# One trunk layer on one Trainium2 core: weights times values of both attentions in two matmuls instead of three, halves added by an accumulating DMA

## The chip, the cores and the metric

The kernel runs on one core of a Trainium2 chip. The metric is the device time of one execution in microseconds (us), the median of three runs. The profile is taken from one further execution by the hardware profiler; its times count from the start of its own span. The engines are PE (TensorE; PEld is its weight load), DVE (VectorE), ACT (ScalarE), POOL (GpSimd) and SP (SyncE, which here only issues DMAs).

## The reference, cut to what matters

One decoder layer over 1024 positions: an input projection, four mixers side by side (a state space model, "fox" attention with forgetting, RWKV-7, "sb" stick-breaking attention), a gated merge of the four, an output projection, an MLP. The two attentions are:

```python
# both: 4 heads of 64, S = 1024, query blocks of 128
def _forgetting_attention(q, k, v, f_logit):           # "fox"
    logits = einsum('bqhd,bkhd->bhqk', qb, kf) * scale
    logits = logits + c[query] - c[key]                # c: running sum of log-sigmoid(f_logit)
    probs = softmax(where(kpos <= qpos, logits, -inf))
    return einsum('bhqk,bkhd->bqhd', probs, vf)

def _stick_breaking_attention(q, k, v):                # "sb"
    z = einsum('bqhd,bkhd->bhqk', qb, kf) * scale
    log_rest = where(kpos < qpos, log_sigmoid(-z), 0)
    between = cumsum(log_rest, reverse) - log_rest
    weights = where(kpos < qpos, exp(log_sigmoid(z) + between), 0)
    return einsum('bhqk,bkhd->bqhd', weights, vf)
```

The change is in the last line of each: weights times values.

## The kernel before

Everything is float32 accurate to more bits than one fp32r matmul gives, so each operand is split in two fp32r tiles, a high half (a rounded copy, by ACT) and a low half (the rest, by DVE: `split`), and a product is three matmuls: high by high, low by high, high by low.

The program is one sequence for the PE that a planner in the file (`Driver`) sets: generators emit work, the planner keeps a modelled clock with costs of its own for each engine, and emits what is ready. The PE's order is the order of emission. On DVE and ACT the order is pinned to the planner's modelled start times. SP and POOL, which issue the DMAs and a few memsets, are ordered by the framework. Every engine works its own queue strictly in order. The attentions run in two stages, fox (430 to 591 us of the span) and sb (756 to 939), each with three `worker` generators over 32 items, 4 heads by 8 query blocks (`qb` 7 down to 0). Beside them the PE fills with gate projections and branch merges (`merges`, matmuls named `mm<-t,wh`, `mm<-y,wh` and the like), whose weights ACT and DVE split as they arrive.

One item: scores by PE into PSUM tiles `x` (QS by KH and KL); weights W by DVE and ACT (fox: `ACTIVATE W` is the exponential; sb: ACT writes the sigmoids R and W, DVE scans R); PE transposes W (`x<-cst,W`); ACT writes the high half `PTh`, DVE the low half `WR`; then, for each of the `qb + 1` key blocks, three matmuls into `y[0:64]`, 64 array columns wide with 128 columns streamed: Vh by PTh, Vl by PTh, Vh by WR. ACT copies the sum to `yst` (a pool of two buffers), and SP stores it to `SCR["Y"]` (`scr_Y`) in DRAM, which the merges read back as `wr<-scr_Y`. In sb, POOL writes a single 1 behind each R row (`MEMSET R`).

In the planner's model a DMA reads nothing that is held: `issue("d", ..., outs, [], ...)` has an empty list of inputs, so it takes a `yst` buffer to be free when ACT has written it. On the chip the copy two later waits until the DMA that reads the buffer has landed. A store costs the planner's model `outs[0].nbytes() / 3.6e5 * (1 + more)` on its one DMA resource, with `more` set for an accumulating DMA.

Of the kernel before, what the change touches and what calls it, by code (L numbers as in the profile page):

```python
# [9 lines left out]
F32 = mybir.dt.float32  # L10
F32R = mybir.dt.float32r
BF16 = mybir.dt.bfloat16
AF = mybir.ActivationFunctionType
ALU = mybir.AluOpType
AX = mybir.AxisListType

P = 128
# [299 lines left out]
def body(ctx, tc, I, O, dbg=None):  # L317
    nc = tc.nc
    drv = Driver()
    V, A, G, SY = (Timed(e, drv, k, tc) for e, k in ((nc.vector, "v"), (nc.scalar, "a"), (nc.gpsimd, "g"), (nc.sync, "s")))  # L320
# [22 lines left out]
    def nm(s):  # L343
        uid[0] += 1
        return f"{s}_{uid[0]}"
# [15 lines left out]
    def px():  # L361
        return ps.tile([P, 512], F32, tag="x", name=nm("x"), bufs=5)
# [21 lines left out]
    def split(dst_h, dst_l, src):  # L384
        A.copy(dst_h, src)
        V.tensor_tensor(out=dst_l, in0=src, in1=dst_h.bitcast(F32), op=ALU.subtract)
# [186 lines left out]
    SCR = {}  # L573
# [424 lines left out]
    def attn(pool, which):  # L998
        fox = which == 0
        ops, left = {}, [8] * 4  # L1000
# [6 lines left out]
        made, count = {}, [0] * 4  # L1007

        def operands(tag):
            def stage():  # L1010
                return wpool.tile([P, 512], F32, tag=tag, name=nm("st"), bufs=NRAW if tag == "wr" else 1)
            while jobs and (tag or jobs[0][0] == 0):
                hd, k = jobs.pop(0)
                while hd >= 2 and left[hd - 2]:
                    yield None
                if hd not in made:
                    made[hd] = [pool.tile([P, S], F32R, tag=t, name=nm(t), bufs=2) for t in ("QS", "KH", "KL")]
                    made[hd] += [pool.tile([P, 8, 64], F32R, tag=t, name=nm(t), bufs=2) for t in ("Vh", "Vl")] + [None]
                    if fox:
                        made[hd][5] = pool.tile([P, S], F32, tag="cb", name=nm("cb"), bufs=2)  # L1020
                        G.dma_start(out=made[hd][5], in_=SCR["c"][hd].partition_broadcast(P))
                QS, KH, KL, Vh, Vl, cb = made[hd]
                ct, o64 = hd // 2, (hd % 2) * 64
                if k < 4:
                    h = (0, 1, 1, 0)[k]
                    hs = slice(h * 512, (h + 1) * 512)
                    src = SCR["qk"][which * 4 + ct + 2 * (k % 2 == 0)]
                    t = pool.tile([P, 512], F32, tag="PTh", name=nm("raw"), bufs=4) if hd == 0 else stage()
                    for half in (0, 64):
                        SY.dma_start(out=t[half:half + 64], in_=src[o64:o64 + 64, hs])  # L1030
                    yield 0.1
                    if k % 2 == 0:
                        split(KH[:, hs], KL[:, hs], t)
                    else:
                        A.activation(out=QS[:, hs], in_=t, func=AF.Copy, scale=0.125)
                        V.scalar_tensor_tensor(out=QS[64:128, hs], in0=t[64:128], scalar=0.125, in1=QS[64:128, hs].bitcast(F32),
                                               op0=ALU.mult, op1=ALU.subtract)
                elif fox:
                    t = stage().rearrange("p (a d) -> p a d", d=64)
                    SY.dma_start(out=t, in_=SCR["v"].rearrange("(a p) d -> p a d", p=P)[:, :, hd * 64:hd * 64 + 64])  # L1040
                    yield 0.1
                    split(Vh, Vl, t)
                else:
                    h = k - 4
                    t = stage()[0:64]
                    SY.dma_start(out=t, in_=SCR["qk"][8 + ct, o64:o64 + 64, h * 512:(h + 1) * 512])
                    yield 0.1
                    o = px()
                    for tb in range(4):
                        T.transpose(o[:, tb * 64:(tb + 1) * 64], t[:, tb * P:(tb + 1) * P], ident[0:64, 0:64])  # L1050
                    hv = slice(h * 4, h * 4 + 4)
                    split(Vh[:, hv].rearrange("p a d -> p (a d)"), Vl[:, hv].rearrange("p a d -> p (a d)"), o[:, 0:256])
                count[hd] += 1
                yield 0.1
                if count[hd] == (5 if fox else 6):
                    ops[hd] = made[hd]
            if not jobs:
                ws.cap = NRAW

        def worker():  # L1060
            for n, hd, qb in items:
                while hd not in ops or turn[0] < n:
                    yield None
                QS, KH, KL, Vh, Vl, cb = ops[hd]
                ct, o64 = hd // 2, (hd % 2) * 64
                L = (qb + 1) * P
                qsl = slice(qb * P, (qb + 1) * P)
# [12 lines left out]
                for n0 in range(0, L, 512):  # L1080
                    n1 = min(L, n0 + 512)
                    o = px()
# [27 lines left out]
                for g0 in range(0, qb + 1, 4):  # L1110
                    o = px()
# [3 lines left out]
                WR = pool.tile([P, S if L > 512 else 512], F32R, tag="W" + sz, name=nm("WR"), bufs=2)  # L1115
# [6 lines left out]
                y = px()  # L1122
                for kb in range(qb + 1):
                    ph = pth[kb // 4][:, kb % 4 * P:kb % 4 * P + P]
                    T.matmul(y[0:64, 0:P], lhsT=Vh[:, kb, :], rhs=ph, start=kb == 0, stop=False)
                    T.matmul(y[0:64, 0:P], lhsT=Vl[:, kb, :], rhs=ph, start=False, stop=False)
                    T.matmul(y[0:64, 0:P], lhsT=Vh[:, kb, :], rhs=WR[:, kb * P:(kb + 1) * P], start=False, stop=kb == qb)
                free["W" + sz] += 1
                free["P"] += (L + 511) // 512
                yst = pool.tile([64, P], F32, tag="yst", name=nm("yst"), bufs=2)  # L1130
                A.copy(yst, y[0:64, 0:P])
                SY.dma_start(out=SCR["Y"][1 if fox else 3, ct, o64:o64 + 64, qsl], in_=yst)
                left[hd] -= 1
                if not any(left):
                    finished["fox" if fox else "sb"] = True
# [2 lines left out]
        for tag in ("st", "wr", None, None, None):  # L1138
            drv.add(operands(tag), 1)
        for _ in range(3):  # L1140
            drv.add(worker(), 0)
# [1099 lines left out]
```

## Time and profile before

| | us |
|---|---|
| median of 3 runs (lowest, highest) | 1870.84 (1868.87, 1873.22) |
| the profiled execution: its own time | 1872.88 |
| the profiled execution: its span | 1871.1 |
| PE busy in the span | 1815.3 (97%) |
| fox stage, first 130 us (430 to 560): PE busy | 126.61 |
| sb stage (756 to 945, 189 us): PE busy, DVE busy | 181.20, 154.79 |

The profiled execution's own time is 1.8 us above its span and 2.0 above the median. Busy time of a PE matmul counts from its start to a modelled end, so neighbouring matmuls overlap: the distance between two starts is what one costs in a dense run. "Idle before" in square brackets at a row's end is the engine's wait and what ended it.

### The profile page before, as it was taken

The page shows a single profiled execution, that of the slowest core. Times are in us where ns is not written, and L with a number is a line of the kernel's source. Part 1 is how long each engine was busy: PE and PEld are TensorE (multiplying, and loading weights), DVE is VectorE, ACT ScalarE, POOL GpSimd, SP SyncE. Part 2 cuts the span into 40 slices and gives each one's busy share as a digit, 9 for nine tenths or more (in the row PEclk, how much of TensorE's full clock was granted, in tenths as well). Part 3 has the DMA queues.
Part 4 walks back from the last instruction along what each step waited for, and adds up shares of the span by engine and source line. Part 5 has one row for each costly group of instructions (what it writes and reads, how often), then busy time and mean ns, then how long its engine had stood idle before and what let it go on. Part 6 is the DMA issues. An engine that isn't in the chain of part 4 may idle for free.

```text
span 1871.1 us, 27581 instructions
## 1 busy us (share of the span) xinstructions
PE 1815.3 (97%) x9651; PEld 1479.0 (79%) x9651; DVE 1239.0 (66%) x2596; ACT 717.0 (38%) x1412; POOL 208.5 (11%) x279
## 2 busy tenths in 40 slices
PE   8999999998999999999999998999999999999998
PEld 7877777777888877787877876788888887888876
DVE  8775865616876764688867666766656565866574
ACT  5443343225454212655544125343333343443230
POOL 0331111100000000000000001111111211121000
PEclk9999999999999988999999998999999999999999
DMA  7343223124422412412154128888889898988441
GB/s 254 114 127 102 82 75 95 66 67 143 146 87 81 101 40 59 129 54 70 39 207 150 51 81 226 239 249 231 245 238 251 209 273 258 284 219 220 129 148 46
DMA packets 177948, 275.27 MB, mean 147 GB/s; under 512 B 37760, under 2 KB 59552, under 8 KB 177680
## 3 DMA queue, kind: packets, MB, share of 16 engines
q1 hardware_dynamic: 155488, 226.31, 37.2%
q0 software_dynamic: 22320, 47.18, 12.9%
q8 instruction: 76, 1.25, 0.3%
q14 instruction: 64, 0.52, 0.1%
HBM read 199.76 MB, written 56.89 MB: 137 GB/s over the span
## 4 chain that ended last, share of the span: by engine, by line
PE 58%; DVE 7%; DMA 5%; ACT 2%; issue 1%; SPq 0%; DVEq 0%; ACTq 0%; POOL 0%; POOLq 0%
PE mm L327 28%; PE x L327 28%; DVE R L280 2%; PE x L332 2%; DMA wr<-in_mlp_w2t_dram 1%; DVE sn L280 1%; DVE W L280 1%; DVE tq L280 1%; DMA scr_g<-gs 1%; DVE t L280 1%; DMA wr<-wl 0%; DMA wl<-in_mlp_w_dram 0%; DMA sn<-scr_H 0%; DMA raw<-scr_qk 0%; DVE Z L280 0%
## 5 line engine op out<-in xcount | busy, mean ns | idle before, releaser
L327 PE MATMUL mm<-t,wh 128*128 128x512 f32 x1600 | 512.6, 402 | 3.5 <-ACT th L280 2.2
L327 PEld LDWEIGHTS mm<-t,wh 128*128 128x128 f32 x1600 | 292.7, 190 | 65.6 <-ACT th L280 2.6
L327 PE MATMUL mm<-t,wl 128*128 128x512 f32 x800 | 314.0, 392 | 0.0
L327 PE MATMUL x<-t,wp 128*128 128x512 f32 x1152 | 270.2, 394 | 8.5 <-ACT wp L280 5.0
L327 PEld LDWEIGHTS x<-t,wp 128*128 128x128 f32 x1152 | 218.4, 190 | 57.5 <-ACT wp L280 5.8
L327 PE MATMUL x<-sx,wp 128*128 128x512 f32 x768 | 179.9, 389 | 1.7 <-ACT sx L280 1.5
L327 PEld LDWEIGHTS mm<-t,wl 128*128 128x128 f32 x800 | 151.3, 189 | 33.2
L327 PEld LDWEIGHTS x<-sx,wp 128*128 128x128 f32 x768 | 144.1, 188 | 32.3 <-ACT sx L280 1.9
L280 ACT CAST wh<-wr 128x512 fp32r<-128x512 f32 (+1 forms) x125 | 74.6, 597 | 122.9 <-PE mm L327 93.7
L280 ACT CAST wp<-wr 128x512 fp32r<-128x512 f32 x96 | 59.2, 621 | 139.4 <-DMA wr<-wl 60.5
L280 DVE TENSOR_TENSOR wp<-wr,wp 128x512 fp32r<-128x512 f32 x96 | 65.8, 688 | 69.7 <-ACT wp L280 68.8
L280 POOL TENSOR_TENSOR wl<-wr,wh 128x512 fp32r<-128x512 f32 x50 | 68.9, 1378 | 278.3 <-ACT wh L280 278.1
L327 PE MATMUL mm<-t,wp 128*128 128x512 f32 x384 | 90.1, 390 | 0.0
L327 PE MATMUL mm<-sx,wp 128*128 128x512 f32 x384 | 89.6, 389 | 0.0
L327 PE MATMUL mm<-wo,t 128*128 128x512 f32 x384 | 89.1, 391 | 0.0
L327 PEld LDWEIGHTS mm<-t,wp 128*128 128x128 f32 x384 | 72.5, 189 | 15.3
L327 PEld LDWEIGHTS mm<-sx,wp 128*128 128x128 f32 x384 | 72.1, 188 | 15.0
L327 PEld LDWEIGHTS mm<-wo,t 128*128 128x128 f32 x384 | 71.6, 188 | 14.5
L280 DVE TENSOR_TENSOR wl<-wr,wh 128x512 fp32r<-128x512 f32 (+1 forms) x75 | 47.4, 634 | 36.6 <-ACT wh L280 35.8
L280 DVE TENSOR_TENSOR wp<-wl,wp 128x512 fp32r<-128x512 f32 x64 | 43.8, 688 | 39.6 <-ACT wp L280 39.5
L280 DVE TENSOR_TENSOR wp<-wh,wp 128x512 fp32r<-128x512 f32 x64 | 43.9, 690 | 32.5 <-ACT wp L280 32.5
L280 ACT CAST wp<-wl 128x512 fp32r<-128x512 f32 x64 | 39.5, 620 | 53.5 <-PE x L327 23.9
(380 smaller groups left out, 3207.9 us busy)
## 6 DMA issues: line engine op xcount, KB each, us to landing
wr<-in_w_in_dram SPq DMA_DIRECT2D x110, 256.0 KB
scr_H<-sn SPq DMA_DIRECT2D x100, 256.0 KB
wr<-in_mlp_w_dram SPq DMA_DIRECT2D x84, 256.0 KB
sn<-scr_H SPq DMA_DIRECT2D x84, 256.0 KB
wh<-in_mlp_w_dram SPq DMA_DIRECT2D x56, 256.0 KB
wl<-in_mlp_w_dram SPq DMA_DIRECT2D x56, 256.0 KB
wr<-wl POOLq DMA_DIRECT2D x32, 256.0 KB, 6.2
wl<-wr POOLq DMA_DIRECT2D x32, 256.0 KB, 4.3
```

The source lines that it names most:

```text
L280: r = f(*a, **kw)
L327: return nc.tensor.matmul(out, lhsT=lhsT, rhs=rhs, **kw)
L332: return nc.tensor.transpose(out, in_, idn)
```

## The change

The two value tiles Vh and Vl (64 columns each) become one tile VV of 128 columns, high values left, low values right. PTh is then streamed once against all 128 columns, into all 128 PSUM partitions (0 to 63: Vh by PTh, 64 to 127: Vl by PTh), and WR against the left 64 columns as before. ACT copies 128 partitions instead of 64. SP stores partitions 0 to 63, and a second DMA, issued by POOL with `accum_op=ALU.add`, adds partitions 64 to 127 to the same DRAM rows once the first has landed.

```diff
@@ operands
-                    made[hd] += [pool.tile([P, 8, 64], F32R, tag=t, name=nm(t), bufs=2) for t in ("Vh", "Vl")] + [None]
+                    vv = pool.tile([P, 8, 128], F32R, tag="VV", name=nm("VV"), bufs=2)
+                    made[hd] += [vv[:, :, 0:64], vv[:, :, 64:128], None, vv]
...
-                    split(Vh[:, hv].rearrange("p a d -> p (a d)"), Vl[:, hv].rearrange("p a d -> p (a d)"), o[:, 0:256])
+                    split(Vh[:, hv], Vl[:, hv], o[:, 0:256].rearrange("p (a d) -> p a d", d=64))
@@ worker
                     ph = pth[kb // 4][:, kb % 4 * P:kb % 4 * P + P]
-                    T.matmul(y[0:64, 0:P], lhsT=Vh[:, kb, :], rhs=ph, start=kb == 0, stop=False)
-                    T.matmul(y[0:64, 0:P], lhsT=Vl[:, kb, :], rhs=ph, start=False, stop=False)
-                    T.matmul(y[0:64, 0:P], lhsT=Vh[:, kb, :], rhs=WR[:, kb * P:(kb + 1) * P], start=False, stop=kb == qb)
+                    T.matmul(y[:, 0:P], lhsT=VV[:, kb, :], rhs=ph, start=kb == 0, stop=kb == qb)
+                    T.matmul(y[0:64, 0:P], lhsT=Vh[:, kb, :], rhs=WR[:, kb * P:(kb + 1) * P], start=False, stop=kb == qb,
+                             skip_group_check=True)
                 free["W" + sz] += 1
                 free["P"] += (L + 511) // 512
-                yst = pool.tile([64, P], F32, tag="yst", name=nm("yst"), bufs=2)
-                A.copy(yst, y[0:64, 0:P])
-                SY.dma_start(out=SCR["Y"][1 if fox else 3, ct, o64:o64 + 64, qsl], in_=yst)
+                yst = pool.tile([P, P], F32, tag="yst", name=nm("yst"), bufs=2)
+                A.copy(yst, y[:, 0:P])
+                dst = SCR["Y"][1 if fox else 3, ct, o64:o64 + 64, qsl]
+                SY.dma_start(out=dst, in_=yst[0:64])
+                G.dma_start(out=dst, in_=yst[64:128], accum_op=ALU.add)
```

On POOL the new DMAs stand in the one queue with the memsets of R. This is a stretch of POOL's program early in the sb stage, after the change (before it, the same stretch holds the memsets alone; a number behind a name tells buffers apart):

```order
L280 MEMSET R_8109 128x1
L280 DMA scr_Y<-yst_8103 64x128
L280 MEMSET R_8189 128x1
L280 DMA scr_Y<-yst_8143 64x128
L280 MEMSET R_8219 128x1
L280 DMA scr_Y<-yst_8183 64x128
L280 MEMSET R_8504 128x1
L280 DMA scr_Y<-yst_8213 64x128
L280 MEMSET R_8430 128x1
```

Each accumulating DMA waits there for the store of the same rows, and a memset behind it waits with it.

On ACT the place of the copies among the rest stays as it was for the first head of fox. This is the stretch with its short last blocks, after the change:

```order
L280 COPY yst_4858<-x_4847 128x128
L280 CAST PTh_4868<-x_4862 128x512
L280 CAST wh_4877<-wr_4739 128x256
L280 CAST PTh_4888<-x_4883 128x384
L280 COPY yst_4903<-x_4894 128x128
L280 COPY yst_4925<-x_4918 128x128
L280 ACTIVATE W_4907,sm_4908<-W_4907,sm_4908 128x256
L280 ACTIVATE W_4929,sm_4930<-W_4929,sm_4930 128x128
```

Copies 4903 and 4925 each need a buffer whose last readers are the two DMAs of an item two earlier; the exponentials stand behind them.

From the second head of fox on, the planner's order moves by a few rows on PE, DVE and ACT (sb keeps its order almost wholly). On DVE, where the second head's middle blocks are made ready, it stood like this before (mg is the running merge, WR the low half of the transposed weights):

```order
L280 TENSOR_TENSOR KL_5060<-st_5065,KH_5059 128x512
L280 RECIPROCAL sm_5222<-sm_5222 128x1
L280 TENSOR_SCALAR W_5221<-W_5221,sm_5222 128x512
L280 SCALAR_TENSOR_TENSOR QS_5058<-st_5068,QS_5058 64x512
L280 TENSOR_TENSOR wl_5237<-wr_4905,wh_5236 128x256
L280 SCALAR_TENSOR_TENSOR mg_4372<-th_5105,mm_5115 128x512
L280 SCALAR_TENSOR_TENSOR mg_4373<-th_5243,mm_5247 128x512
L280 TENSOR_TENSOR WR_5267<-x_5259,PTh_5268 128x512
```

And after the change:

```order
L280 TENSOR_TENSOR wl_5193<-wr_4881,wh_5192 128x256
L280 RECIPROCAL sm_5178<-sm_5178 128x1
L280 TENSOR_SCALAR W_5177<-W_5177,sm_5178 128x512
L280 TENSOR_TENSOR KL_5030<-st_5034,KH_5029 128x512
L280 SCALAR_TENSOR_TENSOR QS_5028<-st_5037,QS_5028 64x512
L280 SCALAR_TENSOR_TENSOR mg_4372<-th_5074,mm_5084 128x512
L280 TENSOR_TENSOR WR_5218<-x_5210,PTh_5219 128x512
L280 TENSOR_TENSOR WR_5218<-x_5215,PTh_5222 128x256
```

The split wl moved ahead of W and KL behind it, and the second merge step moved behind the two WR.

## Rows read from the trace of the kernel before

**Rows 1.** From the profile's page: busy time of each engine, and the shares of the chain of work that ended last.

```profile
PE 1815.3 (97%) x9651; PEld 1479.0 (79%) x9651; DVE 1239.0 (66%) x2596; ACT 717.0 (38%) x1412; POOL 208.5 (11%) x279
PE 58%; DVE 7%; DMA 5%; ACT 2%; issue 1%; SPq 0%; DVEq 0%; ACTq 0%; POOL 0%; POOLq 0%
```

**Rows 2.** Busy time by stretch, the fox stage's first 130 us and the sb stage. Columns: the stretch, its length, busy us (instructions) of PE, PEld, DVE, ACT, POOL, the granted PE clock as a share of 2.4 GHz, the DMA share, GB/s.

```profile
430.00:560.00 130.00, 126.61 (x840) 107.62 (x839) 97.11 (x268) 68.34 (x161) 2.17 (x4) 0.97 0.43 129
756.00:945.00 189.00, 181.20 (x1196) 149.28 (x1196) 154.79 (x265) 102.31 (x246) 6.01 (x35) 1.00 0.24 71
```

**Rows 3.** The matmuls of weights times values, by operands. Columns: count, then ns of one (lowest, median, highest), first and last start, and in front of the shape of the streamed operand rows by columns of the array.

```profile
L327 PE MATMUL x<-PTh,Vh x288: 218/222/308, 455.5 to 938.2; 128*64 128x128 f32 x144
L327 PE MATMUL x<-WR,Vh x288: 220/222/308, 455.6 to 938.3; 128*64 128x128 f32 x144
...
L327 PE MATMUL x<-PTh,Vl x288: 220/222/308, 455.5 to 938.3; 128*64 128x128 f32 x144
```

**Rows 4.** PE in order of time: the ends of one run of 24 such matmuls with what stands before and behind it, and the end of another with a pair 128 columns wide behind it. Columns: start, us from start to end, then as above.

```profile
455.24 0.39 PE L327 MATMUL mm<-t,wl 128*128 128x512 f32 x1
455.46 0.22 PE L327 MATMUL x<-PTh,Vh 128*64 128x128 f32 x1
...
456.84 0.22 PE L327 MATMUL x<-WR,Vh 128*64 128x128 f32 x1
456.90 0.45 PE L327 MATMUL x<-KH,QS 128*128 128x512 f32 x1
457.19 0.40 PE L327 MATMUL x<-KL,QS 128*128 128x512 f32 x1
457.42 0.28 PE L327 MATMUL x<-KH,QS 128*128 128x256 f32 x1
...
552.19 0.22 PE L327 MATMUL x<-WR,Vh 128*64 128x128 f32 x1
552.25 0.28 PE L327 MATMUL x<-KH,QS 128*128 128x128 f32 x1
552.36 0.28 PE L327 MATMUL x<-KL,QS 128*128 128x128 f32 x1
552.47 0.69 PE L327 MATMUL mm<-t,wh 128*128 128x512 f32 x2
```

**Rows 5.** DMAs issued by POOL: count, KB of each, median us from issue to landing.

```profile
y<-in_x_dram POOLq DMA_DIRECT2D x8, 512.0 KB, 3.8
scr_v<-vs POOLq DMA_DIRECT2D x8, 128.0 KB, 2.0
cst<-in_consts_dram POOLq DMA_DIRECT2D x1, 144.0 KB, 6.3
```

**Rows 6.** SP's queue at the end of the sb stage: the last two stores of yst, and the first reads of the same rows, which wait for them.

```profile
938.72 1.08 SPq L280 DMA_DIRECT2D scr_Y<-yst  x2
941.24 0.82 SPq L280 DMA_DIRECT2D wr<-scr_Y  x2
```

**Rows 7.** The first head's short blocks in fox, in order of time on SP, ACT and PE: the stores of two items (two issues in one row), the copies two items later, the exponential behind them, and the transposes that need it.

```profile
471.79 1.62 SPq L280 DMA_DIRECT2D scr_Y<-yst  x2
...
475.80 0.26 ACT L280 COPY yst<-x 64x128 f32<-64x128 f32 x1 [0.93 <-PE x L327]
476.62 0.26 ACT L280 COPY yst<-x 64x128 f32<-64x128 f32 x1 [0.56 <-PE x L327]
476.78 0.51 ACT L280 ACTIVATE W<-W,sm 128x256 f32<-128x256 f32 x1
...
478.26 0.38 PE L332 MATMUL x<-cst,W 128*128 128x128 f32 x2
```

**Rows 8.** The same at short blocks of the third head in sb: two stores, the copies two items later, the sigmoid between them, and the transposes.

```profile
886.56 1.23 SPq L280 DMA_DIRECT2D scr_Y<-yst  x2
...
890.12 0.26 ACT L280 COPY yst<-x 64x128 f32<-64x128 f32 x1 [0.29 <-PE x L327]
890.41 0.38 ACT L280 ACTIVATE R<-x 128x256 f32<-128x256 f32 x1
891.64 0.26 ACT L280 COPY yst<-x 64x128 f32<-64x128 f32 x1 [0.57 <-ACT W L280]
...
892.68 0.41 PE L332 MATMUL x<-cst,W 128*128 128x128 f32 x2 [0.26 <-DVE W L280]
```

**Rows 9.** Two of POOL's memsets of R in the same place, with POOL's wait before each.

```profile
888.60 0.10 POOL L280 MEMSET R<- 128x1 f32 x1 [7.68 <-DVE W L280]
892.65 0.10 POOL L280 MEMSET R<- 128x1 f32 x1 [3.95 <-DVE W L280]
```

**Rows 10.** After the sb stage: the split of the branch weights, the matmuls that use them with the sb values read back, and the PE's next wait.

```profile
951.04 0.41 ACT L280 CAST wh<-wr 128x256 fp32r<-128x256 f32 x1 [2.40 <-DMA wr<-in_w_branch_dram]
...
952.77 0.62 PE L327 MATMUL mm<-y,wh 128*128 128x512 f32 x2
...
965.33 0.70 PE L327 MATMUL mm<-y,wh 128*128 128x512 f32 x2 [2.42 <-DVE th L280]
```

**Rows 11.** The PE's longest wait in the fox stage, and the two stretches behind it (columns as in rows 2).

```profile
500.44 1.22 PE L327 MATMUL mm<-y,wh 128*128 128x512 f32 x2 [3.12 <-DVE mg L280]
...
500.00:505.00 5.00, 4.56 (x15) 3.58 (x16) 4.46 (x10) 0.00 (x0) 0.00 (x0) 0.50 0.72 223
505.00:510.00 5.00, 5.00 (x44) 4.66 (x43) 2.35 (x8) 2.40 (x7) 0.00 (x0) 0.83 0.54 151
```

More of the change, by code (lines that the diff above doesn't have):

```diff
@@ L1021, in operands @@
                         G.dma_start(out=made[hd][5], in_=SCR["c"][hd].partition_broadcast(P))
-                QS, KH, KL, Vh, Vl, cb = made[hd]
+                QS, KH, KL, Vh, Vl, cb, _ = made[hd]
                 ct, o64 = hd // 2, (hd % 2) * 64
@@ L1063, in worker @@
                     yield None
-                QS, KH, KL, Vh, Vl, cb = ops[hd]
+                QS, KH, KL, Vh, Vl, cb, VV = ops[hd]
                 ct, o64 = hd // 2, (hd % 2) * 64
```

## The prediction

> **What bounds the kernel now.** I read the page first. PE is busy for 97% of the span and carries 58% of the chain that ended last, more than all other engines together [rows 1]. So a microsecond counts when it is a microsecond of PE: matmuls that take less, or a PE that waits. Then the two stages that the change touches [rows 2]: in the fox stretch PE idles 130 - 126.61 = 3.4 us, in sb 189 - 181.20 = 7.8 us, with DVE at 82%. There is almost no idle time to win back, and what ACT or DVE are late by soon shows on PE, whose order is fixed.
>
> **The matmuls.** The three groups have 288 each, 64 columns wide, 128 streamed [rows 3]. Their 222 ns is a latency. What one costs is the distance of two starts: 24 run from 455.46 to 456.90 [rows 4], 0.060 us each. A key block is 3 x 0.060 = 0.180, all 288 blocks 51.8 us.
>
> After, a block is one matmul 128 columns wide and one 64 wide, both with 128 streamed. The nearest row for the wide one is the score pair KH, KL at 128 streamed: 552.25, 552.36, 552.47 [rows 4], 0.11 each, nearly twice the 64-wide one though it streams as much. So width sets the price here, not the stream. Block: 0.111 + 0.060 = 0.171, saving 0.009 x 288 = **2.6 us**. The ends: if the wide one cost 0.060 as well, 17.3 us saved. If each step from narrow to wide cost extra as it does before a long matmul (456.90 to 457.19 is 0.29, the next 0.23 [rows 4]), 0.06 more a block, 288 x (0.06 - 0.009) = 14.7 us lost. I take 0.171: the short pair behind a narrow run shows 0.06 and 0.11, without an extra.
>
> The Trainium skill speaks against the change twice. "TensorE: Matmul & The Clock Gate", section "LDWEIGHTS (loading the stationary operand)", gives the load as columns over 1.2 ns; as an estimate 53 and 107 ns, so 160 for a block either way, nothing saved. Rows 4 show a little more per matmul than that, 0.060 and 0.11; with nothing saved the sum below is +5.2 instead of +2.6. And "TensorEngine Tiling (Array Packing)", section "Key Properties", says that changing the tiling mode, not just the tile, drains the engine, and the new pair changes width at each matmul. The trace does not show a drain where widths change: 455.24 to 455.46 is 0.22 behind a long matmul, 552.19 to 552.25 is 0.06 [rows 4]. If it drained, 576 changes would each cost the rest of the latency, 0.222 - 0.060, together 93 us.
>
> **ACT's copy and the splits** keep their free size (128 and 512 columns), only partitions and strides change: nothing, and ACT is 38% busy [rows 1] if a few ns were added.
>
> **The accumulating DMA and the two yst buffers.** This is where it can lose. A buffer is free for the copy two later when its last DMA has landed. A store takes about 1.95 us: the second issue of the last pair starts at about 939.3, the read of the same rows goes out at 941.24 [rows 6]. Now the add follows: it waits for that landing, is issued by POOL, and lands. No accumulating DMA is in this trace. Bounds: 2.0 us, a store four times as large from POOL, and 6.3, a load at the kernel's start [rows 5]. An add must read DRAM before it writes, so it lies above the plain store; the read of 512 KB takes 3.8 with its larger transfer. I take 3.0, between those two. So a buffer is held 4.95 us from the store's issue.
>
> Where does that meet a copy? In fox's first head the stores go out at 471.79 and 472.95, so the buffers come free at 476.74 and 477.90; the copies two later ran at 475.80 and 476.62 [rows 7], so they are held by 0.9 and 1.3. In sb's third head a store at 886.56 frees its buffer at 891.51, and the copy at 890.12 [rows 8] is held 1.4. Counted in this way over all 64 copies, seven places are held, by 0.4 to 1.4 us; these two are the first and the last. Together **5.8 us**. At 2.0 two places are left, 0.7 us. At 6.3 each gets 3.3 more and some six others join with about 2: 5.8 + 23 + 12 = 41.
>
> Behind the held copy on ACT wait the exponential (476.78) or the sigmoids (890.41), behind those DVE's work on W, behind that PE's transposes. At 892.68 PE already waits 0.26 us for DVE [rows 8], so a hold there is passed on in full; at 478.26 PE does not wait [rows 7], so some of it is cover. I take four fifths: 4.6 us (ends 0.6 and 33).
>
> **POOL.** Its queue is in order, so memsets of R stand behind adds that wait for their stores. A memset now follows at once on the release of R after waits of 4 to 8 us [rows 9]; the adds ahead of it are due before that release (at 889 the one ahead of 892.65). Nothing; with that cover gone, up to about 2.5 us at each head's end in sb. In fox the loads of cb stand between adds too; each waits for DVE to leave the buffer of two heads earlier, which comes after the adds ahead of it.
>
> **The end of sb.** The read of the finished rows (941.24) waits for the last add, 3 us later, and SP's queue behind it holds the branch weights. Their high half is done at 951.45 and the matmul takes it at 952.77 [rows 10], so 1.3 us are to spare and 1.7 would show. But PE's next wait, 2.42 us at 965.33, is for the gate values th, which do not come from the attention, and takes up most of what PE lost before it. I count a third, **0.6 us** (ends 0 and 3.0). At fox's end the merges that read its rows come much later: nothing.
>
> **The planner.** The matmul terms of its model do not change, but its DMA resource is booked more, and from fox's second head on some rows change places. The longest PE wait of the stage lies there: 3.12 us on a merge step of DVE at 500.44, followed by a granted clock of 0.50 for 5 us and 0.83 for the next [rows 11]. That costs 3.1 + 2.5 + 0.85 = 6.5 us. The new order does the same DVE work ahead of the first merge step, so I count 0, with 6.5 either way.
>
> **Sum:** -2.6 + 4.6 + 0.6 = +2.6 us. On the profiled execution, whose own time is 1872.88, that is 1875.5; it lies 2.0 above the median of the runs, so I forecast **1873.4**, a gain on PE given back by held copies. A difference under 0.2% (3.7 us) can hardly be told from none here.
>
> **The rivals.**
> - *Late add (slower).* The add lands after 4.5 us: seven holds grow by 1.5, some others join with 3 together, 19 us, four fifths of it 15; -2.6 + 15 + 0.6 = +13, 1884. For it: loads from POOL of 3.8 and 6.3 us. Against: the POOL store of 2.0 us, and the add is small. It decides from an add of 3.2 us on, where the net passes 3.7.
> - *No gain on PE.* The block costs what it did: +5.2, 1876.0. Rows 4 leave 9 ns a block, which is little to rely on.
> - *The stall goes.* The new order takes away the wait at 500.44 and the low clock behind it: 1873.4 - 6.5 = 1866.9, with an add of 2.0 us 1862.3. For it: the changed rows are just there. Against: DVE was busy 4.46 of 5 us behind the wait [rows 11], and its work is the same.
> - *A third less.* The wide matmul costs what a narrow one does: -17.3 + 5.2, 1858.7. For it: the same columns are streamed. Against: the pair at 552.25.
> - *A drain at each change of width:* 1873.4 + 93 + 2.6, 1969. Against: the changes in rows 4.
>
> **How the numbers follow.** Forecast 0.42 (1868.8 to 1874.6, nearly all within 0.2%), late add 0.27, no gain 0.05, the stall goes 0.16 (two thirds of it faster by more than 0.2%), a third less 0.07, drain 0.03. Faster: 0.07 + 0.11 = 0.18. Slower: 0.27 + 0.05 + 0.03 and 0.02 from the forecast's upper end, 0.37. Same: 0.45. The range, 1864 to 1887, leaves out the drain, a third less, the lowest of the stall that goes (0.03) and the upper part of the late add (0.07), 0.2 in all.
>
> **What would show it.** Starts of the wide and narrow matmuls 0.17 us apart per block. ACT's copies waiting for DMA scr_Y in some seven places, 0.4 to 1.4 us each, about 5 us after the store of two items before. PE waits for DVE W in sb up from before, by 3 to 4 us. The read of the sb rows 3 us behind its store's landing. POOL's adds landing after about 3 us. I would be wrong if the adds land after more than 4 us, if the distance of starts is not 0.17, or if the wait and the low clock at 500 are gone or have a twin elsewhere.

## The result, and the profile after

The changed kernel takes 1881.61 us (median; 1871.57 to 1891.0), the kernel before, beside it on the same chip, 1872.17 (1857.4 to 1880.94). The ratio is 1.0052, with a 95% interval from 1.0037 to 1.0067: about 9 us slower, inside the range forecast and beyond the 1873.4 that was forecast as likeliest. The profiled execution's own time is 1885.72, its span 1883.9.

The two stages of the change, as in [rows 2], of after:

```profile
430.00:560.00 130.00, 120.29 (x696) 101.07 (x696) 92.95 (x249) 63.43 (x147) 18.77 (x24) 0.97 0.49 133
756.00:945.00 189.00, 175.77 (x1016) 143.87 (x1015) 149.57 (x250) 101.26 (x239) 25.39 (x59) 0.99 0.30 76
```

PE, the first busy column, now idles 9.7 us in the fox stretch and 13.2 in sb, where it idled 3.4 and 7.8. The granted clock, the third column from the right, is what it was to 0.01. So PE isn't slower at its work: it waits more.

One run of weights times values in order of time on PE, of after, which answers to [rows 4] (start, us, then operands, rows by columns of the array, streamed shape):

```profile
459.63 0.39 PE L327 MATMUL mm<-t,wl 128*128 128x512 f32 x1
459.87 0.22 PE L327 MATMUL x<-PTh,VV 128*128 128x128 f32 x1
459.92 0.22 PE L327 MATMUL x<-WR,VV 128*64 128x128 f32 x1
459.98 0.28 PE L327 MATMUL x<-PTh,VV 128*128 128x128 f32 x1
460.09 0.22 PE L327 MATMUL x<-WR,VV 128*64 128x128 f32 x1
...
461.02 0.27 PE L327 MATMUL x<-PTh,VV 128*128 128x128 f32 x1
461.13 0.22 PE L327 MATMUL x<-WR,VV 128*64 128x128 f32 x1
461.19 0.45 PE L327 MATMUL x<-KH,QS 128*128 128x512 f32 x1
```

From 459.98 to 461.19 lie seven blocks, 0.173 us each: 0.11 for the wide matmul, 0.06 for the narrow one. The first wide one of this run costs only 0.05 (459.87 to 459.92); its load had started at 459.64, while the matmul ahead still ran. Over all runs the first wide one costs 0.06 in the median, the others 0.11. Summed, from the first start of each run to the next other matmul, the 288 blocks take 49.5 us; before they took 54.1.

Now ACT's waits over both attentions, of after (us in total, times, longest):

```profile
ACT yst L280 <- DMA scr_Y<-yst: 31.2, 15, 5.7
ACT yst L280 <- PE x L327: 24.4, 21, 2.5
```

The first line did not exist before: in that trace no wait of a yst copy is put down to a DMA. And PE's waits for W in sb (756 to 960), of before and then of after:

```profile
PE x L332 <- DVE W L280: 4.8, 10, 1.0
```

```profile
PE x L332 <- DVE W L280: 9.8, 14, 1.7
```

One hold followed from engine to engine, in sb of after (SP, POOL, ACT, DVE, PE; in brackets the idle time before the row and what ended it):

```profile
896.29 1.23 SPq L280 DMA_DIRECT2D scr_Y<-yst  x2
899.14 0.82 POOL L280 DMA_DIRECT2D scr_Y<-yst  x1 [8.49 <-DVE WR L280]
902.54 0.27 ACT L280 COPY yst<-x 128x128 f32<-128x128 f32 x1 [3.16 <-DMA scr_Y<-yst]
902.70 0.39 ACT L280 ACTIVATE R<-x 128x256 f32<-128x256 f32 x1
903.13 0.29 DVE L280 TENSOR_TENSOR R<-R,cst 128x128 f32<-128x128 f32 x1 [3.16 <-ACT R L280]
904.97 0.41 PE L332 MATMUL x<-cst,W 128*128 128x128 f32 x2 [1.65 <-DVE W L280]
```

The store is issued at 896.29, its add 2.85 us later, and the copy that needs the buffer starts 3.40 us after that. ACT stood 3.16 us at the copy; the sigmoid of the next row behind it came late, DVE stood the same 3.16 us for it, and PE lost 1.65. The profile does not show when a store on SP's queue lands, so the add's row names another engine as the end of its wait. That it waited for its store is read from the program and from the distance, and is tested below, with the add sent to another place.

This hold of 6.25 us is one of the longer ones. The view of the copies and adds has, for the 64 adds (ns to issue: lowest, median, highest) and for their landing:

```profile
L280 POOL DMA_DIRECT2D scr_Y<-yst x64: 812/823/1583, 465.4 to 955.4; - x64
...
DMA to landing us min/median/max: 2.3/2.5/4.6
```

Item by item, the add starts 2.27 to 4.61 us behind its store's issue (median 2.69) and lands 2.27 to 4.64 us behind its own start (median 2.47). From the store's issue to the add's landing it is 4.59 to 8.80 us, with a median of 5.31. A copy that waits starts 0.15 us after that landing.

A measure of the stages by themselves, used below: from the start of the first copy of yst to the start of the last, in fox and in sb, in the profiled execution of each kernel, added. Before it is 133.2 + 151.2 = 284.4 us; after 142.1 + 157.4 = 299.5.

### The profile page after: what moved, and what is told of

Same layout as the page of the kernel before. It is cut to its first block, busy times and chain, and to the rows that moved or that the text cites. A ratio compares the mean times of both kernels' runs of the same rounds, so it can differ in the third digit from the quotient of the medians.

```text
span 1883.9 us, 27202 instructions
## 1 busy us (share of the span) xinstructions
PE 1810.8 (96%) x9363; PEld 1470.2 (78%) x9363; DVE 1238.1 (66%) x2596; ACT 714.8 (38%) x1412; POOL 260.1 (14%) x343
## 5 line engine op out<-in xcount | busy, mean ns | idle before, releaser
L280 POOL DMA_DIRECT2D scr_Y<-yst x64 | 53.9, 888 | 237.1 <-DMA scr_Y<-yst 63.3
```

Of the source, the lines that this page charges most:

```text
L280: r = f(*a, **kw)
```

## The experiments

The theory: what the change loses is the time for which a yst buffer is held by a store and the add behind it, which ACT, then DVE, then PE wait out. The rivals: the adds cost by themselves (GpSimd's queue, their traffic); the planner's new order; the matmuls gain nothing. Every kernel was timed beside the kernel before, and each ratio is to that.

**Four buffers, the same order on every engine.** The room for them comes from two small edits.

```diff
-yst = pool.tile([P, P], F32, tag="yst", name=nm("yst"), bufs=2)
+yst = pool.tile([P, P], F32, tag="yst", name=nm("yst"), bufs=4)
-sm = pool.tile([P, 4], F32, tag="sm", name=nm("sm"), bufs=8)
+sm = pool.tile([P, 4], F32, tag="sm", name=nm("sm"), bufs=8) if fox else None
-R = pool.tile([P, (S if L > 512 else 512) + 32], ...
+R = pool.tile([P, (S if L > 512 else 512) + 8], ...
```

> The changed kernel with four yst buffers instead of two; the order on PE, ACT and DVE is that of the changed kernel. Theory (held copies): ACT's waits for DMA scr_Y before the copies, 30.6 us in the changed kernel, fall under 3 us, the gain on PE (4.6 us by the starts of the two traces) stays, and the time is 1866 to 1871 us, 0.2% under the kernel before. Rival (the planner's new order costs the time): the waits go, the time stays within 1877 to 1884. Rival (the added DMAs cost it by POOL's queue or by traffic): the waits go, the memsets of R are late, the time stays at 1877 to 1884.

Measured: 1867.78 us, ratio 0.9988 (0.9967 to 1.0008), the attentions 282.6 us. The copies wait for PE and hardly for anything else; ACT's line for the copies in the attentions (busy us, mean ns, then idle us ahead: in all, and by what ended it):

```profile
L280 ACT COPY yst<-x 128x128 f32<-128x128 f32 x64 | 17.1, 269 | 45.8 <-PE x L327 44.8 <-ACT yst L280 0.6
```

All 64 adds are still there, issued in the same order. The loss went with the holds.

**No add at all, two buffers, the same order but for some rows of SP's queue.** The product of the weights and the low halves of the values is left out of the result.

```diff
-G.dma_start(out=dst, in_=yst[64:128], accum_op=ALU.add)
+t = drv.book("g", max(drv.ready(yst), drv.free(dst)), 0.5) + 0.6
+drv.issue("d", dst.nbytes() / 3.6e5 * 2, [dst], [], 2.0, False, t)
```

> The changed kernel without the accumulating DMA on the chip: the low halves (Vl by PTh) are computed and copied but left out of the result. The planner still books the DMA, so the order on PE, ACT and DVE is that of the changed kernel, and yst has two buffers. Theory (held copies): a buffer is held by the store alone, some 3 us, and the time is 1866 to 1871. Rival (order): 1877 to 1884. If it is more than 3 us below the kernel with four buffers, the add costs by more than the buffers, at the end of the sb stage or on POOL.

Measured: 1867.59, ratio 0.9972 (0.9953 to 0.9991), the attentions 282.9. That is the time with the adds and four buffers, so 64 adds that hold nobody up cost nothing that can be measured; each of the two ratios is known to about 4 us.

**The planner not told of the add,** so that PE's order is that of before (all but two rows), with two buffers and with four.

```diff
-            if name == "dma_start":
+            if name == "dma_start" and not more:
...
-            else:
+            elif name != "dma_start":
```

> The changed kernel, but its planner does not book the accumulating DMA, so that all but two rows of PE's order (the matmuls of weights times values aside) are those of the kernel before. Two yst buffers, the DMA runs on the chip. Theory (held copies): ACT still waits 20 to 40 us for DMA scr_Y, the time is 1877 to 1885. Rival (order): the time comes back to 1866 to 1873.

> Four yst buffers and the order of the kernel before, with the accumulating DMA. Theory (held copies): 1866 to 1870, within 2 us of the kernel with four buffers and the new order. Rival (order): 4 us or more below that kernel. Rival (POOL's queue or traffic): 1877 to 1884.

Measured: 1894.32 with two buffers, ratio 1.0116 (1.0088 to 1.0143), and 1884.66 with four, 1.0069 (1.0045 to 1.0094). Both are longer than the theory of held copies had put them (1877 to 1885 and 1866 to 1870), and four buffers did not bring the time down to before's. The attentions take 291.8 and 280.9 us, so the holds are worth 11 there in this order too, and four buffers bring them below before's 284.4. The rest of the time is elsewhere. From the last copy of sb to the end these two take 941 and 943 us, before, after and four buffers 931 to 933: with PE's order as before, the rows of SP and POOL behind the attentions had changed places as well, and a load of MLP weights came late (PE's waits from 1600 to 1700 us, four buffers in this order):

```profile
PE x L327 <- ACT wp L280: 5.8, 1, 5.8
```

The profiled executions of the two four-buffer kernels are 25 us apart (1860.95, the shortest of its twelve, and 1886.40, near the longest of its eight); 17 of them lie between the attentions, at a lower clock (below). By the medians the kernels are 17 apart in all. As tests of the order by itself these two runs are inconclusive.

**Three matmuls in the new order, no add.** This is the kernel without the add, with before's three products. It computes all of it.

```diff
-T.matmul(y[:, 0:P], lhsT=VV[:, kb, :], rhs=ph, start=kb == 0, stop=kb == qb)
+T.matmul(y[0:64, 0:P], lhsT=Vh[:, kb, :], rhs=ph, start=kb == 0, stop=False)
+T.matmul(y[0:64, 0:P], lhsT=Vl[:, kb, :], rhs=ph, start=False, stop=False)
...
-A.copy(yst, y[:, 0:P])
+A.copy(yst[0:64], y[0:64, 0:P])
```

> The kernel of e2_no_add (no adding DMA, the order of the changed kernel on every engine) with the three 64-column matmuls of before in each block instead of two: against e2 it differs in the matmuls alone, against the kernel before in the order alone. If a shorter block is worth its length on TensorE: the bursts took 54.11 us before and 49.51 us after, so e2's 1867.6 plus 4.6 is 1872. If the bursts lie off the path (another engine decides when the next copy comes): 1867.6, within 2 us, and the order alone is what stands between it and the kernel before's 1873.

Measured: 1871.42, before 1871.17, ratio 1.0018 (0.9996 to 1.0039). The new order by itself is worth nothing that can be told from zero. Against the kernel with two matmuls it is 3.8 us longer by the medians, though the two ratios, taken beside the kernel before on different chips, would make it 8.6; each is known to 4 us. The attentions, in one profiled execution of each, take 285.5 where that has 282.9: the shorter blocks give 2.6 us there.

**Two and three buffers, with the two small edits of the four-buffer kernel kept.**

> The kernel of e1_four_buffers with two buffers for yst again; what is left against the changed kernel are the two edits that made room for the buffers (24 columns less behind R, and no sm tile in the second attention). If the buffers were what e1 gained by: as the changed kernel, 1881.6 within 3 us, with some 30 us of ScalarE's copies waiting for the adding DMA. If the room-making edits were: 1868, with those waits still there.

> As e1_four_buffers with three buffers. The copies of the four-buffer kernel's trace, put through two buffers that are each held 6.06 us from the copy's end (what the trace of the changed kernel shows), would wait 14 to 30 us in all, by how much of a wait the later copies take over; through three buffers 1.8 us, in three places. Held copies as the cause: 1868 to 1870 us, ScalarE waiting 1 to 4 us for the adding DMA. If the adds cost time by themselves, through GpSimd's queue or by what they move, more buffers don't matter so steeply: 1872 to 1878, between the two.

Measured: with two 1886.07, ratio 1.0079 (1.0048 to 1.0109), the attentions 301.9; with three 1867.34, 0.9988 (0.9962 to 1.0014), the attentions 284.0. Two buffers come out 4.5 us above the changed kernel's 1881.61, outside the 3 us expected, but above it and not at 1868. So the edits that made room are not what helped. The copies in the attentions, two buffers and then three:

```profile
L280 ACT COPY yst<-x 128x128 f32<-128x128 f32 x64 | 17.3, 270 | 72.9 <-PE x L327 29.2 <-DMA scr_Y<-yst 26.8 <-issue 13.2
```

```profile
L280 ACT COPY yst<-x 128x128 f32<-128x128 f32 x64 | 17.1, 268 | 49.4 <-PE x L327 42.1 <-issue 2.2 <-DMA scr_Y<-yst 1.8
```

26.8 us of waiting for the add become 1.8, the sum expected for a hold of 6.06 us over three buffers, though in one place and not in three. PE's waits for W in both attentions fall with it, from

```profile
PE x L332 <- DVE W L280: 15.2, 19, 2.3
```

to

```profile
PE x L332 <- DVE W L280: 6.3, 13, 1.0
```

**One buffer.**

> As e6_two_buffers_control with a single buffer, so that every copy waits for the add of the copy before. The copies of the four-buffer trace, put through one buffer in order, each wait pushing all that follow: held 6.06 us, 154 us later at the end (1868 + 154 = 2022); held 4.95 us, which the prediction took, 108 us (1976); held 3.3 us, were store and add side by side, about 50 (1918). If buffers aren't what the changed kernel lost by: near 1882 to 1900.

Measured: 2013.92 (two runs), ratio 1.0748 (1.0698 to 1.0798), the attentions 430.3 us, 148 more than with four buffers. A hold of 6.06 us was to give 154, one of 4.95 108, one of 3.3 about 50. ACT's waits:

```profile
ACT yst L280 <- DMA scr_Y<-yst: 171.3, 39, 7.2
```

Held by one DMA alone, the buffer would have cost about 50, so both hold it. The run does not show 6.06 us to be the length: in these 39 places the next copy starts 4.73 to 8.33 us after the end of the one before, 5.6 in the mean.

**The add to another place than the store,** so that it no longer waits for the store to land.

```diff
-G.dma_start(out=dst, in_=yst[64:128], accum_op=ALU.add)
+z = SCR["Z"][nz[0] % 8]
+if nz[0] < 8:
+    G.dma_start(out=z, in_=yst[64:128])
+else:
+    G.dma_start(out=z, in_=yst[64:128], accum_op=ALU.add)
+nz[0] += 1
```

> The changed kernel with two buffers, but each add goes to one of eight scratch rows of its own instead of the place of the store (the first eight as plain writes that fill them), so that an add no longer waits for its store to land; left out of the result: the low halves' products with the weights. As many DMAs are issued, of the same size, on the same queues. If the hold is store and add one after the other (2.8 to 3.3 us to the add's start, then 3.24): the buffer is held about 3.3 us, the copies of the four-buffer trace would then wait under 1 us through two buffers, and the time is that with four buffers, 1868. If the add is slow by itself (its issue on GpSimd, its traffic, landing behind other transfers): as the changed kernel, 1880 to 1886, with 25 us or more of ScalarE's copies waiting for it.

Measured: 1870.24, ratio 0.9986 (0.9965 to 1.0007), the attentions 281.6; PE, ACT and DVE keep the changed kernel's order but for a few rows. ACT's copies:

```profile
L280 ACT COPY yst<-x 128x128 f32<-128x128 f32 x64 | 17.2, 269 | 50.7 <-PE x L327 27.4 <-issue 14.5 <-DMA scr_Y<-yst 3.5
```

An add now starts 0.27 us behind its store's issue in the median, not 2.69, and takes as long to land as before (2.54, where it was 2.47). Two buffers are enough when the two DMAs run side by side. It is the chain, store and then add, that holds a buffer too long, and neither link alone.

**The sum on VectorE.**

```diff
+V.tensor_tensor(out=yst[0:64], in0=yst[0:64], in1=yst[64:128], op=ALU.add)
 SY.dma_start(out=dst, in_=yst[0:64])
-G.dma_start(out=dst, in_=yst[64:128], accum_op=ALU.add)
```

> Two matmuls as in the changed kernel, but the halves are added on VectorE in SBUF (64 more adds of 64x128) ahead of a single store; no adding DMA, two buffers, and the order is the planner's own for this. If only the held buffers cost: the time of e2 and e1, 1868, give or take the 7 us that an order has been worth. If VectorE decides the pace of the attentions: each add is some 0.2 us, 64 of them 13 us, and up to half of them ahead of a W that TensorE waits for, 1872 to 1880, with TensorE's waits for W up by as much.

Measured: 1890.24, ratio 1.011 (1.0083 to 1.0137), above both expectations; the attentions take 300.8 us. The 64 adds are 18.4 us of DVE:

```profile
L280 DVE TENSOR_TENSOR yst<-yst 64x128 f32<-64x128 f32 x64 | 18.4, 288 | 13.8 <-ACT yst L280 12.2
```

No copy waits for a DMA, and the stages are as long as with two held buffers. PE's waits in them, of this kernel:

```profile
PE mm L327 <- DVE mg L280: 8.7, 4, 4.0
PE x L332 <- DVE W L280: 8.7, 15, 1.3
PE mm L327 <- DVE wl L280: 2.8, 1, 2.8
```

All three are DVE's. Before, the first was 3.1 us and the second 4.8, and the third did not show. How much of the 16 us by which the attentions are longer than before is the adds, and how much the planner's order, which is another one here, was not taken apart.

## Why the prediction was right and where it was off

Slower by 9 us was inside the range, and held copies are the cause, as the prediction had it. But the time lies above the forecast's own 1868.8 to 1874.6, near the 1884 of the rival of the late add, and that rival's condition did not come: it wanted adds that land after 4.5 us, and the median is 2.47, with one of 64 above 4. So it is in part luck that the range took the time in. Of the signs of being wrong that were named none appeared; the sign that told was the copies' waits, 15 of up to 5.7 us where seven of up to 1.4 were forecast. Point by point:

- **The matmuls: right.** Starts 0.17 us apart per block were forecast, 0.173 is there, and 2.6 us of gain; the stages without the adds give 2.6 (285.5 against 282.9). PE's time in the blocks fell by more, 4.6; most of the excess lies in the first matmul of each run, where a wide one costs 0.06 and not 0.11 in the median, and it did not reach the stages. Widths change at every matmul, and the starts stay 0.11 and 0.06 us apart, with no room for the 0.16 us that a drain was priced at. The Trainium skill's rule ("TensorEngine Tiling (Array Packing)", section "Key Properties") on changes of the tiling mode is not seen to apply to a change of width.
- **The hold: the first of two steps that were off.** The prediction put 4.95 us from the store's issue to the free buffer, 1.95 for the store and 3.0 for the add, the same for every item. The trace has 2.85 and 3.40 in the rows at 896.29. In fox it has 2.82 and 3.24, with the store at 475.62:

```profile
475.62 1.87 SPq L280 DMA_DIRECT2D scr_Y<-yst  x2
478.44 1.72 POOL L280 DMA_DIRECT2D scr_Y<-yst  x2 [9.43 <-ACT wh L280]
481.68 0.27 ACT L280 COPY yst<-x 128x128 f32<-128x128 f32 x1 [2.80 <-DMA scr_Y<-yst]
```

  That is 6.06 us, and the median of all 64 is 5.31 to the landing. The add was sized too long, 3.0 where the median is 2.47. The store was sized too short: its 1.95 came from one read on SP's own queue at the quiet end of sb [rows 6], while an add on POOL starts 2.69 us behind the store's issue in the median and never less than 2.27. The two errors nearly cancel in the median; what one hold for all leaves out are the long ones, up to 8.80. For the add, the Trainium skill ("DMA: Bandwidth & Descriptors", section "Anatomy of one DMA — SWDGE (gpsimd) path") has 2.0 us and the bytes over 436 GB/s, as an estimate 2.1 us for 32 KB; the trace's 2.47 is above that; the page has no figure for an adding transfer.
- **From the hold to the wait: the second.** Forecast were 5.8 us in seven places, measured 31.2 in 15. Recounted on the trace before by the prediction's own rule, 13 copies are held, by 8.7 us; its 5.8 counts two neighbours once and leaves out holds under 0.3. The copies of the four-buffer trace, put through two buffers at the same 4.95 us from the store's issue, would wait 14 to 22 us in 13 to 17 places, by how much of a wait the later copies take over; at the hold that each item has in that trace it is 24 to 48 us in 14 to 26. So the forecast went by copies that come later behind the stores than those of the changed kernel do, and by a hold without its long cases. The late-add rival's 19 us were too few for its own hold as well: with neighbours counted once the trace before gives 25 us at that hold (1.95 + 4.5), and the rival did not let a held copy push the next ones on ACT.
- **What is passed on.** Four fifths were forecast. The stages are 17 us longer than with four buffers (299.5 against 282.6) at 31.2 us of waiting, a little over half; by the medians, 1881.6 against 1867.8, it is 14.
- **POOL and the end of sb: nothing to be seen.** Nothing was forecast for POOL and 0.6 us for the end of sb. With four buffers the adds stay on POOL and cost nothing. The sb rows are read at 958.08, 5.6 us behind the last pair's first store (952.50) where it was 2.5 before [rows 6], so the 3 us of delay came; still the time from the last copy to the end is 931.4 us, 932.5 before.
- **The planner's order: right.** PE's long wait on the merge step stayed, 3.88 us at 507.22 with a clock of 0.69 for 505 to 510, and the order alone made 1.0018.

```profile
507.22 1.22 PE L327 MATMUL mm<-y,wh 128*128 128x512 f32 x2 [3.88 <-DVE mg L280]
...
505.00:510.00 5.00, 2.78 (x11) 0.69 0.75 191
```

The sum as measured: about -3 from the matmuls, 0 from the order, +14 from held copies where 4.6 had been put. That is 11, and 9 were measured.

No kernel that computes everything came out measurably below before: with three or four buffers the interval takes in 1, and the 2.6 us of the matmuls in the stages is what there is to win.

## What to carry to other kernels

Before a second DMA is chained to a store, work out how long the staging buffer is then held, from the store's issue to the landing of the last one, in the busy part of the stage, with its long cases and not by one row, and put the times at which the trace asks for buffers through it: a hold just above the distance of the copies is steep, and one buffer more was the cure here. Time that comes free on the busiest engine is worth only what its stage can pass on, here a little over half (2.6 of 4.6 us). An addition moved to an engine that is not the bound can still sit in the chain which the bound waits for; VectorE's 64 adds came with longer waits of PE for DVE, though the order changed with them.

## What the runs showed of the hardware that had not been expected

- A DMA that adds into DRAM, 64 x 128 floats issued by POOL, took 0.82 us to issue and 2.47 us in the median to land (2.27 to 4.64). Ordered behind a plain store to the same place, it landed 4.59 to 8.80 us after the store's issue (median 5.31). Sent to another place, with no store to wait for, it took as long to land (median 2.54).
- The same matmuls can take different times. The four-buffer kernel and the two-buffer kernel with its edits have one order on PE, and from fox's last copy to sb's first they take 185.3 and 192.2 us; the four-buffer kernel in before's order, which differs there in a few rows, takes 202.0. From 640 to 756 us PE is busy to the same 113.2 us in both four-buffer kernels, the one in the new order and the one in before's:

```profile
640.00:756.00 116.00, 113.22 (x554) 1.00 0.30 88
```

```profile
640.00:756.00 116.00, 113.23 (x490) 0.87 0.22 65
```

  At a mean clock of 0.87 it gets through 490 matmuls, at 1.00 through 554. What sets the clock there these runs do not show.
- In the 20 runs of the changed kernel the spans spread by 5.4 us (standard deviation); each span times its own mean clock spreads by 1.7. Most of what differs from run to run goes with the mean clock.
